# Two or one expert matrices in a ring slot instead of four slices, in a mixture-of-experts block on one core

## The chip, the core and the metric

One core of one Trainium2 chip runs the kernel as a single launch. The metric is device time in microseconds (us) of one execution; the median of three runs before the change is 612.62 us.

## What is computed

A residual stream `x` of 256 tokens by 1024 goes through a mixer, then through a mixture of 32 experts (top group, then two of its eight experts), then through a gated embedding and a final norm. All of it is float32. The part that the change touches is the mixture:

```python
for g in range(N_GROUPS):
    a = jnp.einsum('td,edf->tef', t, w_gate[g])
    b = jnp.einsum('td,edf->tef', t, w_up[g])
    hid = jax.nn.silu(a) * b * comb[:, g, :, None]
    y = y + jnp.einsum('tef,efd->td', hid, w_down[g])
```

Each expert has three matrices of 2 MB: gate and up are 1024 x 512, down is 512 x 1024. All 32 experts are read, 201 MB of the 225 MB that the kernel moves.

## The kernel before, in words

The 32 experts are worked on in eight **quads** of four (`QE`, `NQ`, lines 25 and 26). Up to 32 tokens of an expert stand in a block of 32 columns (`CAP`), so that the four experts of a quad fill 128 columns. A quad needs its gate weights (G), then its up weights (U), then its down weights (D), 8 MB each.

**Loads.** `load_w(q, i)` (line 430) fills one slot of 16 KB per partition, 2 MB in all, by one DMA: i = 0 to 3 are the gate slots, 4 to 7 the up slots, 8 to 11 the down slots. Before the change a slot holds all four experts of the quad, and of each expert two of the eight rows of a partition (`c:c + 2`, line 437), or one of four rows for down (line 439): in memory 4 KB in one run for each partition and expert. The loads go out on the queue of SyncE (SP), in program order. Slots come from the pool `ring` with six buffers (line 38); only the up slots of quad 0 lie elsewhere (pools `xr` and `x4`). A load waits on SP until the products that read its slot's earlier content are done. Two other users take slots of the ring: `wpp` (line 776), loaded after quad 2's down weights and read by the products of line 791, which follow quad 3's down products; and the gate matrix of the embedding (`load_gate`, line 657), which after quad 6 keeps two of the six slots to the end.

**Products.** `proj` (line 619) issues four products, one for each expert j, each into its own 32 columns of TensorE, so that the four run side by side. `gate_up` (line 624) calls it for c = 0 to 7, slot by slot: eight products (16 matmul records in the trace, since a float32 product leaves two) as soon as one slot has landed, and that slot is free after them. A matrix set is 32 products. `down` (line 647) does the same with four slots. After the gate products follow the up products, `hidden` and `hidden_t` (the activation and its transposes, `ph`), the down products, `combine` (the products `py`) and `spread` (the transposes `pc`). The gather of the next quad (`pgx`) lies between.

```python
for i in range(4):
    w = get_w(q, i0 + i).rearrange("p (e c f) -> p e c f", e=QE, c=2)
    for k in range(2):
        c = 2 * i + k
        proj(o, xg, c, w[:, :, k], c == 0, c == KC - 1)
    if filler:
        filler(i0 + i)
```

**Order around the change.** After quad 1's down loads, three gate loads of quad 2 are issued ahead (line 742, the third on the queue of GpSimd), and then comes a branch (line 747) that all engines pass, for rounds that these inputs don't need. In quad 7 the `filler` (line 716) puts the embedding's products `gate_x` between the expert products, and the down weights come by columns (`load_chunk`, line 823), which the change leaves alone.

Of the kernel before, what the change touches and what calls it, by code (L numbers as in the profile page):

```python
# [20 lines left out]
KC = D // P  # L21
FE = 512
NE = 32
CAP = 32
QE = 4
NQ = NE // QE
EPS = 1e-6
GELU_C = 0.044715
# [4 lines left out]
def hymba_conv_sgu_hmoe_block(ctx, tc, a):  # L33
    nc = tc.nc
# [19 lines left out]

# [1 line left out]
    sig0 = keep.tile([P, 1], F32, name="sig0")  # L56
# [29 lines left out]
    def keep_warm(n):  # L86
        pb = bank("warm")
        for _ in range(n):
# [6 lines left out]
                   allow_small_or_imprecise_dtypes=True)  # L95
    # lower[i, j] = 1 for j < i
    lower = keep.tile([P, 8, 8], F32, name="lower")
# [26 lines left out]

# [1 line left out]
    fy = tc.alloc_tile_pool(name="fy", bufs=1, side="left")  # L126
# [18 lines left out]
    load_in(1)  # L145
    # rows: g_sgu 0:4, w_conv 4:16, g_ple 16:24
    stage = fz.tile([24, P], F32, name="stage")
# [29 lines left out]

    # exact two-part splits of the weights, two pieces ahead of their products
    nsp = [0]
# [15 lines left out]

    # h^T, d = p * 8 + c, split in two exact parts
    hh = fz.tile([P, KC, NT * P], F32R, name="hh")
# [73 lines left out]
    vn = []  # L271
# [14 lines left out]

    # small parameters, spatial weights
    pst = bank("pst")
# [35 lines left out]

    # spatial mixing: mT[ch, t] = g_sgu[ch] * sum_s ws[t, s] vn[s, ch] + b[head, t]
    mT = fz.tile([P, 4, 256], F32, name="mT")
# [16 lines left out]
    def post_u():  # L343
        for i in range(2):
            gu = fz.tile([P, 512], F32, tag="g", name="gu", bufs=4)
            gelu(gu, pz_u[i])
            y = fz.tile([P, 512], F32, tag="g", name="yu", bufs=4)
            nc.vector.tensor_tensor(y, gu, mT[:, 2 * i:2 * i + 2].rearrange("p j n -> p (j n)"), op=OP.mult)
            put_y(4 + 2 * i, y)
        # router weights with the gain of the norm, bias on every partition  # L350
        gff3 = gffn.unsqueeze(2)
        pin(nc.vector.tensor_tensor(wr[:, :, 0:4], wgr, gff3.to_broadcast([P, KC, 4]), op=OP.mult))
        for g in range(4):
            pin(nc.vector.tensor_tensor(wr[:, :, 4 + 8 * g:12 + 8 * g], wrr[:, g],
                                        gff3.to_broadcast([P, KC, 8]), op=OP.mult))
        pbias = bank("pbias")
        nc.tensor.matmul(pbias[:, 0:36], ones_f, rb, start=True, stop=True)
        nc.vector.tensor_copy(biasB, pbias[:, 0:36])
# [16 lines left out]

# [1 line left out]
    po = [[bank("po", "L") for _ in range(2)] for _ in range(NT)]  # L377
# [48 lines left out]

# [1 line left out]
    wtiles = {}  # L428

    def load_w(q, i, queue=nc.sync):  # L430
        pool = ring if q or i < 4 or i > 7 else xr if i < 7 else x4
        w = slot(f"we{q}_{i}", pool)
        es = slice(q * QE, (q + 1) * QE)
        if i < 8:
            src = w_gate if i < 4 else w_up
            c = 2 * (i % 4)
            queue.dma_start(w.rearrange("p (e c f) -> p e c f", e=QE, c=2), src[:, es, c:c + 2, :])
        else:
            queue.dma_start(w.rearrange("p (e d) -> p e d", e=QE), w_down[:, es, i - 8, :])
        return w  # L440

    def get_w(q, i):
# [3 lines left out]

# [1 line left out]
    plog = bank("plog", "L")  # L448
# [17 lines left out]
    for t in range(NT):  # L466
        # normalized rows, d = p * 8 + c laid out as [c, p]
        nc.scalar.activation(h2[:, t].rearrange("t c p -> t p c"), xs[:, t].rearrange("t (p c) -> t p c", c=KC),
                             AF.Copy, scale=stat[:, 8 + t:9 + t])
    keep_warm(24)  # L470
    x4 = tc.alloc_tile_pool(name="x4", bufs=1, side="right")

# [1 line left out]
    gl = lg[:, :, 0:4]  # L474

    def ranks(v, n, name):
        """How many come before each of the n values: larger ones, or equal ones at a lower index."""
        shape = [P, NT, n, n]
        mine, other = v.unsqueeze(3).to_broadcast(shape), v.unsqueeze(2).to_broadcast(shape)
        gt = mp.tile(shape, F32, tag="gt", name="gt" + name)  # L480
        eq = mp.tile(shape, F32, tag="eq", name="eq" + name)
        nc.vector.tensor_tensor(gt, other, mine, op=OP.is_gt)
        nc.vector.tensor_tensor(eq, other, mine, op=OP.is_equal)
        nc.vector.tensor_tensor(eq, eq, lower[:, 0:n, 0:n].unsqueeze(1).to_broadcast(shape), op=OP.mult)
        nc.vector.tensor_tensor(gt, gt, eq, op=OP.add)
        rank = mp.tile([P, NT, n], F32, name="rank" + name)
        nc.vector.tensor_reduce(rank, gt, axis=AX.X, op=OP.add)
        return rank
# [61 lines left out]

    # combine weights
    gm = rout[:, :, 0:1]
# [33 lines left out]
    for t in range(NT):  # L586
        nc.vector.tensor_tensor(comb[:, t].rearrange("p (g e) -> p g e", g=4),
                                ohg[:, t].unsqueeze(2).to_broadcast([P, 4, 8]),
                                inner[:, t].unsqueeze(1).to_broadcast([P, 4, 8]), op=OP.mult)
    # rounds beyond the first that the fullest expert needs  # L590
    cmax = stat[:, 10:11]
# [5 lines left out]
    nc.vector.tensor_copy(nover, over[0:1, 7:8])  # L597
# [1 line left out]
    def hidden(pg, pu):  # L599
# [16 lines left out]
    def rows(j):  # L616
        return slice(j * CAP, (j + 1) * CAP)

    def proj(o, xg, c, w, first, last, placed=lambda i: i):
        for j in range(QE):  # L620
            placed(nc.tensor.matmul(o[rows(j)], xg[:, c, rows(j)], w[:, j], start=first, stop=last,  # L621
                                    tile_position=(0, j * CAP)))

    def gate_up(q, xg, filler=None):
        pg, pu = bank("pg"), bank("pu")
        for o, i0 in ((pg, 0), (pu, 4)):
            for i in range(4):
                w = get_w(q, i0 + i).rearrange("p (e c f) -> p e c f", e=QE, c=2)
                for k in range(2):
                    c = 2 * i + k  # L630
                    proj(o, xg, c, w[:, :, k], c == 0, c == KC - 1)
                if filler:
                    filler(i0 + i)
        return hidden(pg, pu)
# [12 lines left out]
    def down(q, hT, cm):  # L647
        pd = [bank("pd", "L") for _ in range(2)]
        for i in range(4):
            w = get_w(q, 8 + i).rearrange("p (e d) -> p e d", e=QE)  # L650
            for h in range(2):
                proj(pd[h], hT, i, w[:, :, h * 512:(h + 1) * 512], i == 0, i == 3)
        combine(pd, cm)

    # w_ple_gate, d = c * 128 + p, in two exact parts, and the gate's products with x as the first
    # seven quads leave it
    def load_gate():
        for i in range(2):
# [6 lines left out]
            for c in range(4):  # L665
                f = slice(c * D, (c + 1) * D)
                # with the gain of the norm before it
                g = cols[:, 16 + 4 * i + c:17 + 4 * i + c]
                nc.scalar.activation(hi[:, f], w[:, f], AF.Copy, scale=g)
                nc.vector.scalar_tensor_tensor(wlo[:, 4 * i + c], w[:, f], g, hi[:, f].bitcast(F32),  # L670
                                               op0=OP.mult, op1=OP.subtract)
# [34 lines left out]
    for q in range(NQ):  # L706
        if q:
            cm = spread(q, d)
        if q + 1 == NQ:
            # one token at most in each slot: its weight, and where it goes  # L710
            cmf = cm.rearrange("s t n -> s (t n)")
# [26 lines left out]
        if q == 1:  # L738
            # further rounds of CAP tokens per expert, as many as the fullest expert needs
            for i in range(3):  # L740
                # the loop uses no software queue, so nothing there waits for the last of these
                wtiles[q + 1, i] = load_w(q + 1, i, nc.gpsimd if i == 2 else nc.sync)
# [28 lines left out]
        if q == 2:  # L771
            # p @ w_ple_proj
            pq = tc.alloc_tile_pool(name="pq", bufs=1, side="right")
# [22 lines left out]

# [1 line left out]
    # The last quad's down weights arrive by columns.  # L798
    q = NQ - 1
# [83 lines left out]
    steps = {"D": down_chunk, "T": transposed, "Y": to_tokens, "S": gate_slots}  # L883
    # The columns' stages, so ordered that TensorE has products of one while another's are prepared.
    for step in "D0 T0 Y0 S0 D1 S1 T1 Y1 S2 D2 S3 T2 Y2 D3 S4 T3 Y3 D4 S5 T4 Y4 S6".split():
# [43 lines left out]
    added(*a11)  # L929
    # the gain goes on this half before its scale is known  # L930
    pin(nc.gpsimd.tensor_tensor(xs[:, 1, a10[2]], xs[:, 1, a10[2]], gF[:, a10[2]], op=OP.mult))
# [34 lines left out]
```

## Time and profile before

| What | Value |
|---|---|
| Median of three runs | 612.62 us (612.23 to 612.63) |
| Profiled execution, first to last instruction | 612.1 us |
| TensorE busy | 456.3 us (75%), 2955 matmul records |
| VectorE, ScalarE, GpSimd busy | 25%, 17%, 7% |
| Moved by DMA | 225.07 MB in 70600 packets, mean 368 GB/s |
| Mean granted TensorE clock | 0.871 of 2.4 GHz |

The span of the profiled execution stands 0.5 us under the median of the runs. The page cuts the span into 40 slices of 15.3 us; a digit is the busy share of a slice in tenths. In the rows of a timeline the first number is the start, the second the duration, and a bracket at the end tells how long the engine was idle before and what ended it.

### The profile page before, as it was taken

The numbers are of one execution on the slowest core, as the hardware profiler recorded it, in microseconds if no ns is written. First come the engines' busy times: TensorE is split into PE (matmuls) and PEld (weight loads), VectorE is DVE, ScalarE is ACT, GpSimd is POOL, SyncE is SP. The second block draws the span as 40 slices with busy tenths as digits, with TensorE's granted clock in tenths as the row PEclk, the third lists the DMA queues.
The fourth block names the chain that finished last, engine by engine and source line by source line (L and its number), as shares of the span: only waits on it lengthen the run. The fifth ranks groups of instructions, "written<-read, shape, count | busy, mean of one in ns | idle before, by whom it ended". The sixth has DMA issues, their size and how long they took to land.

```text
span 612.1 us, 6928 instructions
## 1 busy us (share of the span) xinstructions
PE 456.3 (75%) x2955; PEld 235.2 (38%) x2955; DVE 150.2 (25%) x275; ACT 101.9 (17%) x171; POOL 45.9 (7%) x42
## 2 busy tenths in 40 slices
PE   8999999989764775565657965756575676799891
PEld 8799988643310121121312331203110311356571
DVE  2647854422010201020012001200120012601236
ACT  4543545010000000000001200000000003300243
POOL 1543440000000000000000000000000000000003
PEclk9999999999875798788887998779877957899996
DMA  8997669699999799999999999999999999999921
GB/s 323 354 391 300 243 264 408 242 413 403 408 411 408 293 414 408 407 409 410 409 409 410 409 409 410 408 409 409 410 409 409 409 410 409 408 410 380 322 72 69
DMA packets 70600, 225.07 MB, mean 368 GB/s; under 512 B 3204, under 2 KB 15268, under 8 KB 70564
## 3 DMA queue, kind: packets, MB, share of 16 engines
q1 hardware_dynamic: 70036, 222.48, 93.3%
q0 software_dynamic: 528, 2.10, 0.9%
q8 instruction: 24, 0.39, 0.3%
q14 instruction: 12, 0.10, 0.0%
HBM read 223.52 MB, written 1.05 MB: 367 GB/s over the span
## 4 chain that ended last, share of the span: by engine, by line
DMA 43%; PE 19%; issue 1%; ACT 1%; DVE 1%; POOL 1%; POOLq 0%; SPq 0%; ACTq 0%
DMA we<-in_w_up_dram 17%; DMA we<-in_w_down_dram 16%; DMA we<-in_w_gate_dram 10%; PE pd L621 3%; PE pu L621 3%; PE pg L621 3%; PE pgg L688 1%; PE pgg L689 1%; PE py L644 1%; PE pj L791 1%; PE pgg L690 1%; PE pgg L880 1%; PE pyw L810 1%; PE pyw L811 1%; PE pyw L812 1%
## 5 line engine op out<-in xcount | busy, mean ns | idle before, releaser
L621 PE MATMUL pd<-we,hT 128*32 128x512 f32 x448 | 77.5, 833 | 45.4 <-DMA we<-in_w_down_dram 34.4
L621 PE MATMUL pu<-we,xg 128*32 128x512 f32 x512 | 70.9, 682 | 47.1 <-DMA we<-in_w_up_dram 47.1
L621 PE MATMUL pg<-we,xg 128*32 128x512 f32 x512 | 70.4, 690 | 27.4 <-DMA we<-in_w_gate_dram 27.4
L621 PEld LDWEIGHTS pd<-we,hT 128*32 128x32 f32 x448 | 14.5, 132 | 101.7 <-DMA we<-in_w_down_dram 59.1
L621 PEld LDWEIGHTS pu<-we,xg 128*32 128x32 f32 x512 | 15.2, 118 | 90.5 <-DMA we<-in_w_up_dram 47.2
L621 PEld LDWEIGHTS pg<-we,xg 128*32 128x32 f32 x512 | 15.8, 120 | 72.7 <-issue 36.9
L113 POOL TENSOR_TENSOR stat<-stat,mhalf 128x1 f32<-128x1 f32 (+1 forms) x9 | 6.0, 662 | 430.7 <-ACT yw L816 410.6
L249 PE MATMUL pz<-hh,wh 128*128 128x256 f32 x128 | 36.3, 283 | 0.7 <-ACT g L262 0.7
L251 PE MATMUL pz<-hl,wh 128*128 128x256 f32 x128 | 36.0, 281 | 0.0
L252 PE MATMUL pz<-hh,wl 128*128 128x256 f32 x128 | 35.9, 281 | 0.0
L530 PEld LDWEIGHTS pgx<-d,h 128*128 128x128 f32 x256 | 29.5, 192 | 11.1 <-issue 9.9
L530 PE MATMUL pgx<-d,h 128*128 128x128 f32 x256 | 31.7, 280 | 1.9 <-DVE d L519 1.9
L644 PE MATMUL py<-ys,cm 128*128 128x512 f32 x56 | 29.0, 662 | 2.8 <-DVE ys L639 2.8
L613 ACT ACTIVATE hT<-ph 128x512 f32<-128x512 f32 x8 | 4.8, 597 | 155.1 <-PE ph L611 155.1
L639 DVE COPY ys<-pd 128x512 f32<-128x512 f32 x7 | 4.8, 691 | 104.8 <-PE pd L621 104.8
L604 DVE TENSOR_TENSOR hp<-sg,pu 128x512 f32<-128x512 f32 x8 | 8.2, 1031 | 88.7 <-PE pu L621 88.7
L602 DVE TENSOR_TENSOR sg<-sg,pg 128x512 f32<-128x512 f32 x8 | 5.5, 688 | 97.6 <-ACT sg L601 97.6
L249 PEld LDWEIGHTS pz<-hh,wh 128*128 128x128 f32 x128 | 24.1, 188 | 1.1 <-ACT g L262 0.9
L252 PEld LDWEIGHTS pz<-hh,wl 128*128 128x128 f32 x128 | 24.1, 188 | 0.0
L251 PEld LDWEIGHTS pz<-hl,wh 128*128 128x128 f32 x128 | 24.1, 188 | 0.0
L638 ACT ACTIVATE ys<-pd 128x512 f32<-128x512 f32 x7 | 4.2, 597 | 110.4 <-PE pd L621 110.4
L601 ACT ACTIVATE sg<-pg 128x512 f32<-128x512 f32 x8 | 4.8, 598 | 101.0 <-PE pg L621 101.0
(233 smaller groups left out, 576.1 us busy)
## 6 DMA issues: line engine op xcount, KB each, us to landing
we<-in_w_up_dram SPq DMA_DIRECT2D x32, 2048.0 KB, 22.3
we<-in_w_gate_dram SPq DMA_DIRECT2D x31, 2048.0 KB, 18.5
we<-in_w_down_dram SPq DMA_DIRECT2D x28, 2048.0 KB, 24.0
wd<-in_w_down_dram SPq DMA_DIRECT2D x12, 512.0 KB, 9.3
wo<-in_w_out_dram SPq DMA_DIRECT2D x2, 2048.0 KB
wpg<-in_w_ple_gate_dram SPq DMA_DIRECT2D x4, 1024.0 KB
w_v<-in_w_in_dram SPq DMA_DIRECT2D x4, 512.0 KB, 7.3
w_c<-in_w_in_dram SPq DMA_DIRECT2D x2, 1024.0 KB
```

The costliest lines, as they stand in the source:

```text
L249: nc.tensor.matmul(o, wh[:, s], hh[:, c], start=(c == 0 and j % 2 == 0), stop=False, skip_group_check=True)
L251: nc.tensor.matmul(o, wh[:, s], hl[:, c], start=False, stop=False, skip_group_check=True)
L252: nc.tensor.matmul(o, wl[:, s], hh[:, c], start=False, stop=last, skip_group_check=True)
L530: nc.tensor.matmul(pg[:, c * P:(c + 1) * P], h2[:, t, 4 * i + c], d[:, t].rearrange("p e s -> p (e s)"), start=(t == 0), stop=(t == NT - 1))
L604: nc.vector.tensor_tensor(hp.rearrange("s c p -> s p c"), sg.rearrange("s (p c) -> s p c", c=4), pu.rearrange("s (p c) -> s p c", c=4), op ...
L621: placed(nc.tensor.matmul(o[rows(j)], xg[:, c, rows(j)], w[:, j], start=first, stop=last, tile_position=(0, j * CAP)))
L644: nc.tensor.matmul(py, cm[:, t], ys[:, f], start=True, stop=True)
L688: nc.tensor.matmul(pgg[t][h], hi[:, s], wh[:, f], start=first, stop=False)
L689: nc.tensor.matmul(pgg[t][h], hi[:, s], wl[:, f], start=False, stop=False)
L690: nc.tensor.matmul(pgg[t][h], lo[:, s], wh[:, f], start=False, stop=last)
L791: nc.tensor.matmul(pj, pT[:, c, t * P:(t + 1) * P], wv[:, c, f], start=(c == 0), stop=(c == 1))
L810: pin(nc.tensor.matmul(pyw[h], yh_, wh[:, f], start=(k == 0), stop=False))
```

## The change

A table `PER` gives each quad the number of experts in a slot: two for quads 0, 6 and 7, one for quads 1 to 5. With two, a slot holds four rows c of each expert (two for down), 8 KB in one run; with one, a slot holds the whole matrix of one expert, 16 KB in one run. Number and size of the loads, their order and the number of products stay. A new generator `granules` hands out the rows c in order, each with its four experts' weights: with two experts to a slot it takes two slots at a time, with one it takes all four. `proj` takes a list of four weights. The filler is called at the same places as before. Comments were dropped too.

```diff
+PER = [2] + [1] * (NQ - 3) + [2] * 2
...
     def load_w(q, i, queue=nc.sync):
         pool = ring if q or i < 4 or i > 7 else xr if i < 7 else x4
         w = slot(f"we{q}_{i}", pool)
-        es = slice(q * QE, (q + 1) * QE)
+
+        EP = PER[q]
+        CP = KC // EP
+        g, n = divmod(i % 4, QE // EP)
+        es = slice(q * QE + n * EP, q * QE + (n + 1) * EP)
         if i < 8:
             src = w_gate if i < 4 else w_up
-            c = 2 * (i % 4)
-            queue.dma_start(w.rearrange("p (e c f) -> p e c f", e=QE, c=2), src[:, es, c:c + 2, :])
+            c = CP * g
+            queue.dma_start(w.rearrange("p (e c f) -> p e c f", e=EP, c=CP), src[:, es, c:c + CP, :])
         else:
-            queue.dma_start(w.rearrange("p (e d) -> p e d", e=QE), w_down[:, es, i - 8, :])
+            c = CP // 2 * g
+            queue.dma_start(w.rearrange("p (e c d) -> p e c d", e=EP, c=CP // 2), w_down[:, es, c:c + CP // 2, :])
         return w
+
+    def granules(q, i0, c_slot):
+
+        EP = PER[q]
+        for g in range(EP):
+            ws = [get_w(q, i0 + g * (QE // EP) + n).rearrange("p (e c f) -> p e c f", e=EP, c=c_slot)
+                  for n in range(QE // EP)]
+            for k in range(c_slot):
+                yield g * c_slot + k, [ws[j // EP][:, j % EP, k] for j in range(QE)]
...
-            placed(nc.tensor.matmul(o[rows(j)], xg[:, c, rows(j)], w[:, j], start=first, stop=last,
+            wj = w[j] if isinstance(w, list) else w[:, j]
+            placed(nc.tensor.matmul(o[rows(j)], xg[:, c, rows(j)], wj, start=first, stop=last,
                                     tile_position=(0, j * CAP)))
...
         for o, i0 in ((pg, 0), (pu, 4)):
-            for i in range(4):
-                w = get_w(q, i0 + i).rearrange("p (e c f) -> p e c f", e=QE, c=2)
-                for k in range(2):
-                    c = 2 * i + k
-                    proj(o, xg, c, w[:, :, k], c == 0, c == KC - 1)
-                if filler:
-                    filler(i0 + i)
+            for c, w in granules(q, i0, KC // PER[q]):
+                proj(o, xg, c, w, c == 0, c == KC - 1)
+                if filler and c % 2:
+                    filler(i0 + c // 2)
...
-        for i in range(4):
-            w = get_w(q, 8 + i).rearrange("p (e d) -> p e d", e=QE)
+        for i, w in granules(q, 8, 4 // PER[q]):
             for h in range(2):
-                proj(pd[h], hT, i, w[:, :, h * 512:(h + 1) * 512], i == 0, i == 3)
+                proj(pd[h], hT, i, [r[:, h * 512:(h + 1) * 512] for r in w], i == 0, i == 3)
```

## Rows read from the trace of the kernel before

**Rows 1.** The page, busy tenths in 40 slices of the span.

```profile
PEclk9999999999875798788887998779877957899996
DMA  8997669699999799999999999999999999999921
GB/s 323 354 391 300 243 264 408 242 413 403 408 411 408 293 414 408 407 409 410 409 409 410 409 409 410 408 409 409 410 409 409 409 410 409 408 410 380 322 72 69
```

**Rows 2.** The page, the chain that ended last, by engine.

```profile
DMA 43%; PE 19%; issue 1%; ACT 1%; DVE 1%; POOL 1%; POOLq 0%; SPq 0%; ACTq 0%
```

**Rows 3.** Products of TensorE, timeline, quad 3's gate and up, and quad 2's up.

```profile
274.08 3.38 PE L621 MATMUL pg<-we,xg 128*32 128x512 f32 x16 [3.08 <-DMA we<-in_w_gate_dram]
279.21 1.92 PE L621 MATMUL pg<-we,xg 128*32 128x512 f32 x16 [1.75 <-DMA we<-in_w_gate_dram]
284.33 3.38 PE L621 MATMUL pg<-we,xg 128*32 128x512 f32 x16 [3.20 <-DMA we<-in_w_gate_dram]
...
224.22 1.92 PE L621 MATMUL pu<-we,xg 128*32 128x512 f32 x16 [3.20 <-DMA we<-in_w_up_dram]
```

**Rows 4.** DMA packets: whole span, 32 to 42, 350 to 450, 562 to 570 us.

```profile
DMA packets 70600, 225.07 MB, mean 368 GB/s; under 512 B 3204, under 2 KB 15268, under 8 KB 70564
...
DMA packets 1976, 3.87 MB, mean 387 GB/s; under 512 B 709, under 2 KB 717, under 8 KB 1975
...
DMA packets 10286, 40.92 MB, mean 409 GB/s; under 512 B 306, under 2 KB 306, under 8 KB 10282
...
DMA packets 2803, 2.78 MB, mean 348 GB/s; under 512 B 86, under 2 KB 2803, under 8 KB 2803
```

**Rows 5.** Timeline, SP's loads: quad 3 down; `wpp`; the first after quad 0's products.

```profile
287.79 19.10 SPq L439 DMA_DIRECT2D we<-in_w_down_dram  x4
...
246.39 1.29 SPq L777 DMA_DIRECT2D wpp<-in_w_ple_proj_dram  x1
...
118.49 2.08 SPq L439 DMA_DIRECT2D we<-in_w_down_dram  x2
```

**Rows 6.** Issue to landing: `we` in 350 to 450; issues of 60 to 70, 118 to 119.

```profile
DMA to landing us min/median/max: 23.8/24.0/24.1
...
we<-in_w_gate_dram SPq DMA_DIRECT2D x1, 2048.0 KB, 8.6
...
we<-in_w_down_dram SPq DMA_DIRECT2D x1, 2048.0 KB, 8.8
```

**Rows 7.** Timeline of TensorE, products in a row: quad 0's gate, quad 2's gate.

```profile
116.51 7.07 PE L621 MATMUL pg<-we,xg 128*32 128x512 f32 x64
...
210.27 0.66 PE L543 MATMUL pc<-ident,d 128*128 128x128 f32 x2 [4.11 <-PEq L747]
210.86 7.71 PE L621 MATMUL pg<-we,xg 128*32 128x512 f32 x48
```

**Rows 8.** Stretches of 1 us: engines' busy time, then PEclk, DMA share, GB/s.

```profile
529.00:530.00 1.00, 1.00 (x9) 0.14 (x2) 1.00 (x1) 0.00 (x0) 0.00 (x0) 0.66 1.03 414
530.00:531.00 1.00, 0.96 (x9) 0.73 (x9) 0.66 (x4) 0.38 (x1) 0.00 (x0) 1.00 1.01 401
```

**Rows 9.** Timeline of TensorE after quad 3's down products, 325 to 341 us.

```profile
333.59 7.13 PE L791 MATMUL pj<-wpp,pT 128*128 128x512 f32 x16 [0.69 <-ACT pT L785]
```

**Rows 10.** Timeline, end of quad 1: last down products, the next load on SP.

```profile
199.23 3.27 PE L621 MATMUL pd<-we,hT 128*32 128x512 f32 x16 [5.81 <-SPq L747]
...
210.39 0.40 SPq L437 DMA_DIRECT2D we<-in_w_gate_dram  x1
```

**Rows 11.** The chain that ended last, in order of time, quad 7.

```profile
509.48 16.81 DMA we<-in_w_gate_dram
526.42 3.51 PE pg L621 x16
...
534.03 1.85 PE pg L621 x16
...
548.51 1.85 PE pu L621 x16
```

## The prediction, on record before the run

> **What bounds the kernel now.** I read the page first. Its slices show DMA as the resource that is never off from about 122 to 550 us: the busy digit is 9 and the rate 403 to 414 GB/s in every slice but one [rows 1]. The chain agrees: 43% of the span is DMA, 19% TensorE [rows 2]. The timeline then shows how that looks inside a quad: eight products every 5.12 us (274.08, 279.21, 284.33), each group after a wait for its weights [rows 3]. 5.12 us is what one load of 2048 KB takes at 409 GB/s [rows 4]. SP issues a load as soon as a slot is free: quad 3's first down load starts at 287.79 [rows 5], 0.1 us after the eight gate products at 284.33 end (3.38 us) [rows 3]. So one slot is being read, up to five are in flight, and a load lands 24.0 us after its issue [rows 6], more than four loads' time. This lead keeps DMA busy through branch-free quads. The end is different: from 526.42 on TensorE works almost without a wait, and the quad 7 gate load that lands there sets when this stretch begins [rows 11].
>
> **What the change does to a load.** Bytes, loads, order and products are the same. Packets get longer. Three stretches have loads with runs of 1, 2 and 4 KB: 348, 387 and 409 GB/s [rows 4]. On each of 16 engines a packet then takes 47.1, 84.7 and 160 ns, so 37.6 ns for each KB and 9.5 ns beside it. By this line 8 KB take 310 ns and 16 KB 611 ns: a load takes 4.96 us in quads 6 and 7 and 4.88 us in quads 1 to 5, in place of 5.12. Ends: 5.12 (no gain beyond 4 KB) and 4.80 (nothing beside the 37.6 ns). I take the line, because three rows lie on it. Were all else hidden, this would be 60 loads by 0.24 and some 20 by 0.16, about 17 us.
>
> **What it does to the slots.** With one expert to a slot no product but the first three can run before the fourth slot has landed, since every row c needs all four experts in order. And no slot is free before the last four of the 32 products. So four of six slots stand full while the burst runs, and only two loads are in flight. The count from the landing of the fourth load:
>
> The burst. 32 products at full clock took 7.1 us in quad 0 [rows 7]. But now TensorE waits over 10 us before each burst. After a wait of 4.11 us (ahead of two transposes), 24 products of quad 2 took 7.71 us, so 32 take 9.5 (7.71 and a quarter of 7.07) [rows 7]. After 3.79 us of wait, at 526.42 [rows 11], the clock stood at half until 529.7 (0.66 in the mean over 529 to 530, then 1.00) [rows 8]; 3.3 us at half rate cost 1.6 us, which gives 8.7. Ends: 7.1 and 13.5 (four groups at the 3.38 us of a cold one [rows 3]). I take 8.7 rather than 9.5, since a wait of 3.20 us was once followed by a group at full speed, 1.92 us at 224.22 [rows 3]. The Trainium skill ("TensorE: Matmul & The Clock Gate", HAM oscillation) says that a DMA wait between groups of products sends the clock back to half and that every group then starts cold. By that rule it is 8.7 to 9.5 in each burst; by the row at 224.22 alone it would be 7.1 and the sum below 22.7 us less.
>
> The restart. A load that met an empty queue landed 8.6 and 8.8 us after its issue [rows 6], 3.5 us beyond its 5.12; with the shorter transfer 8.4.
>
> Six slots free for experts: loads one and two are in flight. The first expert's slot is free 0.7 us before the burst ends, so load three goes out at 8.0, lands at 16.4, and load four at 21.3. Before, four loads took 20.5. Each handover from one matrix set to the next costs **0.8 us** instead of gaining 1.0. There are ten: G to U and U to D of quads 1, 2, 4 and 5, and D to G of 4 to 5 and 5 to 6: 8.0.
>
> Five slots: `wpp` is loaded behind quad 2's down weights (issue at 246.39 [rows 5]) and is read until 340.7 by products that follow quad 3's down products [rows 9]. Through quad 3 one slot is gone. Then one load is in flight at the burst, and two, three and four follow it: 8.0, 16.4, 21.3, 26.1. Each costs **5.7 us**; G3 to U3, U3 to D3 and D3 to G4: 17.1. In D2 to G3 the 1.25 MB of `wpp` and the embedding input (3.2 us) lie in the queue too: 26.1 against 23.7 before, 2.4.
>
> **The other parts.** Quad 0 with two to a slot: the ring's first slot is free after 16 products, not eight, 119.6 instead of 118.49 [rows 5], with DMA idle; quad 1's first two loads win half of it back: 0.6. Quad 1's end: 32 products instead of eight lie between the last down load and the branch, 5.4 us more (8.7 against 3.27), and the third early load, on GpSimd's queue, now waits for that burst. But the eight products at 199.23 came after a wait of 5.81 us for the branch and not for data [rows 10], and the longer burst uses up that time. Ends 0 and 5.4; I take 0.5, because the row shows the cover. If the cover is gone, the load at 210.39 [rows 10] and all behind it are that much later. Quad 6: eight loads by 0.16 in the two handovers left, minus 1.3. Quad 7: its first products now need two landed slots, not one, so the stretch at 526.42 begins one load later, plus 5.0. Two slots of the ring are gone there too: the first pair is free at 535.9 (534.03 and 1.85 [rows 11]) plus 5.0, its successors land 8.4 and 5.0 later, at 554.3, and the up products want them at 548.51 plus 5.0: 0.8 late. Together 5.8. SP's own issue times (19.10 us for four loads [rows 5]) shrink with the packets and stay behind DMA; `proj`'s list adds no instruction: nothing.
>
> **Sum.** 8.0 + 17.1 + 2.4 + 0.6 + 0.5 - 1.3 + 5.8 = 33.1 us. The profiled span is 612.1, which makes 645.2; the median stands 0.5 above the span: **646 us**.
>
> **Rivals.**
> *Slot of `wpp` not in the way* (its products moved ahead, into quad 3's waits). For: TensorE will have 10 us waits there, and the gather `pgx` is already placed between up groups. Against: before, `pj` came only after quad 3's down products, though waits of 3 us lay ahead of it [rows 3, 9]. The three handovers fall from 5.7 to 0.8: 14.7 less, 631 us.
> *The longer runs bring nothing*, the change doing half of what it says. Load time 5.12: handovers cost 1.2 and 6.4, D2 to G3 3.1, no gain in quad 6: about 9 more, 655 us. Against it stand the three rates on one line.
> *The clock doesn't come back within a burst.* Burst 13.5: 4.8 more in each of 14 handovers, 713 us. Against: rows 8 show it back after 3.3 us of work.
> *Faster: the two loads in flight outlast the burst.* This happens in the handovers of quads 1 to 6. It decides where the burst takes under 7.9 us (then the fourth load lands within 20.5) and the ring has six slots throughout. At 7.1 each of 13 handovers gains 0.8, and 10.4 less 0.8 (D2 to G3) and 5.6 (the rest) leave a gain of 4.0: 608.6 us. For it speaks the row at 224.22, against it the waits, three times as long as that one, and `wpp`.
>
> **How the numbers follow.** The forecast has 0.54, `wpp` free 0.14, no gain from length 0.13, cold bursts 0.06, faster 0.11, and 0.02 is left for something else. The range runs from the warm burst with `wpp` held (10 us over the span, 622) to the burst of 9.5 with no gain from length (666). It holds `wpp` free and the unchanged rate and leaves out the cold and the faster case, some 0.18. A measurement of this kernel can tell 0.2% from no change. All cases but one are slower: faster 0.11, same 0.03, slower 0.86.
>
> **What would show it.** Packets: 47,104 of 4 KB become 8,192 of 8 KB and 7,680 of 16 KB, so the page should have 39,368. The rate should be near 429 GB/s while two loads are in flight, with a dip once in each 21 us in quads 1 to 5 and a long one, some 6 us, in quad 3. Products should come in groups of 64 records of 8 to 9.5 us. Loads three and four of a set should land 8 to 14 us after issue, not 24. Quad 7's first gate products should wait for a second load. I am wrong if the DMA slices of quads 2, 4 and 5 stay at 9 with over 420 GB/s, if TensorE reads an expert's slot as it lands, or if bursts run at full clock from the start.

## The result, and the profile after

The changed kernel takes 642.78 us (median of four runs, 640.97 to 646.13) against 612.62 us (612.23 to 612.87): a ratio of 1.0503, 95% interval 1.047 to 1.0537. It is slower by 5%, and its runs lie 5 us apart where those of before lie within 0.6 us. The profiled execution has a span of 639.7 us and took 641.43 us.

First the page of the kernel after, the same slices as [rows 1], then its packets and the chain by engine, as [rows 2]:

```profile
PEclk9999999997899789869589898879778986899897
DMA  8997589599999999896787999998999999989911
GB/s 316 346 394 317 200 356 423 221 405 425 364 378 374 423 381 378 349 426 243 326 340 293 428 369 388 421 414 328 389 422 400 421 422 412 421 342 385 329 38 66
DMA packets 39368, 225.07 MB, mean 352 GB/s; under 512 B 3204, under 2 KB 15268, under 8 KB 23460
...
DMA 33%; PE 28%; DVE 2%; issue 1%; ACT 1%; POOL 1%; SPq 0%; POOLq 0%; ACTq 0%; DVEq 0%
```

Before, quads 2 to 6 had one rate, 407 to 414 GB/s. Now single slices reach 421 to 428, above all of before, and beside them stand slices of 243 to 390. DMA got faster while it works and has gaps that it didn't have. In the chain TensorE's share has grown from 19 to 28% and DMA's has fallen from 43 to 33%: some of the time in which weights were moving all along is now spent on products with hardly a load moving beside them.

The timeline of TensorE, kernel after (start, duration, count of records, the wait before):

```profile
218.02 8.32 PE L637 MATMUL pg<-we,xg 128*32 128x512 f32 x57 [2.01 <-DMA we<-in_w_gate_dram]
...
286.58 8.49 PE L637 MATMUL pg<-we,xg 128*32 128x512 f32 x57 [2.98 <-DMA we<-in_w_gate_dram]
...
313.21 9.25 PE L637 MATMUL pu<-we,xg 128*32 128x512 f32 x58 [2.97 <-DMA we<-in_w_up_dram]
...
339.80 7.05 PE L637 MATMUL pd<-we,hT 128*32 128x512 f32 x52 [1.39 <-DMA we<-in_w_down_dram]
...
351.61 7.13 PE L803 MATMUL pj<-wpp,pT 128*128 128x512 f32 x16 [0.69 <-ACT pT L797]
...
493.10 5.90 PE L637 MATMUL pg<-we,xg 128*32 128x512 f32 x26 [4.42 <-DMA we<-in_w_gate_dram]
...
533.50 6.61 PE L637 MATMUL pd<-we,hT 128*32 128x512 f32 x24 [2.09 <-DMA we<-in_w_down_dram]
```

In quads 1 to 5 nearly all 64 records of a set now stand in one burst that begins with the landing of the fourth load; the groups of 16 every 5.12 us [rows 3] are gone. (493.10 and 533.50 are sets of quad 6, with two experts to a slot.) Around the burst of 286.58 the stretches of 3 us (busy times, then granted clock, DMA share, GB/s) and SP's issues read:

```profile
287.00:290.00 3.00, 3.00 (x17) 0.59 (x13) 0.00 (x0) 0.00 (x0) 0.00 (x0) 0.50 0.79 339
290.00:293.00 3.00, 3.00 (x32) 0.92 (x28) 0.00 (x0) 0.00 (x0) 0.00 (x0) 0.94 0.03 11
293.00:296.00 3.00, 3.00 (x25) 1.04 (x18) 0.00 (x0) 0.46 (x1) 0.00 (x0) 1.00 0.31 66
296.00:299.00 3.00, 3.00 (x30) 3.00 (x28) 0.69 (x1) 0.13 (x1) 0.00 (x0) 1.00 0.82 317
```

```profile
294.69 1.28 SPq L442 DMA_DIRECT2D we<-in_w_up_dram  x3
296.06 1.36 SPq L445 DMA_DIRECT2D we<-in_w_down_dram  x1
```

DMA stands at 11 and 66 GB/s for 6 us while TensorE works at full load. SP issues the next loads at 294.69, as the burst ends (286.58 + 8.49 = 295.07) and its first slot comes free. The first 3 us of the burst run at 0.50, the lower level of the clock. The three up loads issued there landed 8.7, 13.2 and 17.6 us later, not 24 [rows 6].

To see where the time went I compare the landing of the same last load of a set. Here are three groups of the kernel before that begin with one, to be held against 218.02, 493.10 and 533.50 above:

```profile
219.09 1.92 PE L621 MATMUL pg<-we,xg 128*32 128x512 f32 x16 [0.53 <-DMA we<-in_w_gate_dram]
...
468.78 3.32 PE L621 MATMUL pg<-we,xg 128*32 128x512 f32 x16 [2.52 <-DMA we<-in_w_gate_dram]
...
510.97 1.92 PE L621 MATMUL pd<-we,hT 128*32 128x512 f32 x16 [1.56 <-DMA we<-in_w_down_dram]
```

| Stretch, up to the last load of | Before | After | Lost | Predicted |
|---|---|---|---|---|
| start to quad 2 gate | 219.1 | 218.0 | -1.1 | 2.7 |
| to quad 6 gate (12 handovers) | 249.7 | 275.1 | 25.4 | 25.9 |
| to quad 6 down | 42.2 | 40.4 | -1.8 | -1.3 |
| to the end of the span | 101.1 | 106.2 | 5.1 | 5.8 |
| span | 612.1 | 639.7 | 27.6 | 33.1 |

The predicted column is the sum's own terms: 0.6, 0.5 and two handovers in the first line; eight handovers of 0.8, 17.1 and 2.4 in the second.

### The profile page after: what moved, and what is told of

Same layout as the page of the kernel before. It is cut to its first block, busy times and chain, and to the rows that moved or that the text cites. A ratio compares the mean times of both kernels' runs of the same rounds, so it can differ in the third digit from the quotient of the medians.

```text
span 639.7 us, 6928 instructions
## 1 busy us (share of the span) xinstructions
PE 489.0 (76%) x2955; PEld 245.8 (38%) x2955; DVE 149.7 (23%) x275; ACT 101.7 (16%) x171; POOL 45.7 (7%) x42
## 2 busy tenths in 40 slices
DMA packets 39368, 225.07 MB, mean 352 GB/s; under 512 B 3204, under 2 KB 15268, under 8 KB 23460
## 3 DMA queue, kind: packets, MB, share of 16 engines
HBM read 223.52 MB, written 1.05 MB: 351 GB/s over the span
## 4 chain that ended last, share of the span: by engine, by line
DMA 33%; PE 28%; DVE 2%; issue 1%; ACT 1%; POOL 1%; SPq 0%; POOLq 0%; ACTq 0%; DVEq 0%
DMA we<-in_w_down_dram 13%; DMA we<-in_w_gate_dram 11%; DMA we<-in_w_up_dram 9%; PE pg L637 7%; PE pu L637 7%; PE pd L637 7%; DVE wlo L682 1%; PE pgg L702 1%; PE pgg L700 1%; PE pgg L701 1%; PE pgg L892 1%; PE pyw L822 1%; PE pgx L545 1%; PE pyw L823 1%; PE pyw L824 1%
## 5 line engine op out<-in xcount | busy, mean ns | idle before, releaser
L637 PE MATMUL pu<-we,xg 128*32 128x512 f32 x512 | 87.8, 681 | 41.8 <-DMA we<-in_w_up_dram 41.8
L637 PE MATMUL pd<-we,hT 128*32 128x512 f32 x448 | 87.0, 654 | 39.6 <-DMA we<-in_w_down_dram 28.2
L637 PE MATMUL pg<-we,xg 128*32 128x512 f32 x512 | 87.1, 712 | 33.1 <-DMA we<-in_w_gate_dram 33.1
L637 PEld LDWEIGHTS pd<-we,hT 128*32 128x32 f32 x448 | 19.8, 115 | 101.8 <-issue 43.4
L637 PEld LDWEIGHTS pu<-we,xg 128*32 128x32 f32 x512 | 19.9, 123 | 95.3 <-DMA we<-in_w_up_dram 51.2
L637 PEld LDWEIGHTS pg<-we,xg 128*32 128x32 f32 x512 | 19.4, 126 | 91.0 <-issue 45.1
L545 PEld LDWEIGHTS pgx<-d,h 128*128 128x128 f32 x256 | 29.5, 192 | 11.2 <-issue 8.5
L657 PE MATMUL py<-ys,cm 128*128 128x512 f32 x56 | 26.2, 608 | 1.4 <-DVE ys L652 1.4
## 6 DMA issues: line engine op xcount, KB each, us to landing
we<-in_w_gate_dram SPq DMA_DIRECT2D x31, 2048.0 KB, 10.8
```

The lines of the kernel that those rows point to most:

```text
L545: nc.tensor.matmul(pg[:, c * P:(c + 1) * P], h2[:, t, 4 * i + c], d[:, t].rearrange("p e s -> p (e s)"), start=(t == 0), stop=(t == NT - 1))
L637: placed(nc.tensor.matmul(o[rows(j)], xg[:, c, rows(j)], wj, start=first, stop=last, tile_position=(0, j * CAP)))
L657: nc.tensor.matmul(py, cm[:, t], ys[:, f], start=True, stop=True)
```

## The experiments

The theory: a set's slots are held to the end of its burst, so too few loads are in flight, and DMA stands idle from the landing of the last of them until the next set's loads have started up. The rivals: length and order alone cost the time, or the clock does. Times of the kernel before beside these runs are 612.9 to 613.1 us.

**1. Hold the slots without longer runs.** The kernel before, its loads of 4 KB unchanged; in quads 1 to 5 the products of a set go round all four slots, so that none is free before the last round.

```diff
+    def hold(o, xg, cw, first, last):
+        for r in range(4):
+            for i, (c, w) in enumerate(cw):
+                j = (i + r + 1) % 4
+                nc.tensor.matmul(o[rows(j)], xg[:, c, rows(j)], w[:, j], start=first and r == 0,
+                                 stop=last and r == 3, tile_position=(0, j * CAP))
```

> The kernel before, loads and packets unchanged (4 KB runs), but in quads 1 to 5 the 32 products of a set go through all four slots in turn, so that none can start before the fourth slot has landed (but three) and every slot is read until the last four products. Theory (held slots): handovers as in the changed kernel with loads of 5.12 us: 21.7 us in place of 20.5 with six slots (ten times), 25 to 27 us in quad 3 (three times), 3 for wpp's place: 641 to 650 us, DMA gaps in every handover. Rival (the long packets are slow or badly fed): no packet is longer, 612 to 616 us.

659.99 us (651.99 to 661.71), ratio 1.0727 (1.0654 to 1.0799). The rival, that the longer packets are what costs and holding costs nothing, is out: holding alone loses 47 us, more than the whole change. The size was missed. The bursts of quad 2 show by how much:

```profile
222.55 9.10 PE L628 MATMUL pg<-we,xg 128*32 128x512 f32 x58 [5.78 <-DMA we<-in_w_gate_dram]
...
245.95 9.69 PE L628 MATMUL pu<-we,xg 128*32 128x512 f32 x58 [3.40 <-DMA we<-in_w_up_dram]
...
269.49 9.87 PE L628 MATMUL pd<-we,hT 128*32 128x512 f32 x52 [2.08 <-DMA we<-in_w_down_dram]
```

They take 9.1 to 9.9 us, against 8.32, 8.63 and 7.05 us in the same sets of the changed kernel, and the fourth loads are 23.4 and 23.5 us apart. So the loss is the slots', and longer runs are not needed for it.

**2. Give `wpp` a buffer of its own.** The changed kernel, with one line other:

```diff
-            wv = slot("wpp")[:, 0:2048].rearrange("p (c n) -> p c n", c=2)
+            wv = pq.tile([P, 2, D], F32, name="wpp")
```

> The changed kernel, with wpp in a buffer of its own instead of a ring slot. Theory: quad 3's handovers fall from 26.6, 26.6 and 24.8 us to about 21.5, some 14 us, and a little at D2 to G3: 625 to 631 us. Rivals (packets, or TensorE's clock alone): loads, packets and products are the same, 640 to 645 us.

630.81 us (626.82 to 632.66), ratio 1.0283 (1.0237 to 1.0329): 12.0 us less than the changed kernel, where the prediction's rival had 14.7 for three handovers. Quad 3:

```profile
286.17 8.22 PE L637 MATMUL pg<-we,xg 128*32 128x512 f32 x57 [2.98 <-DMA we<-in_w_gate_dram]
...
307.42 9.97 PE L637 MATMUL pu<-we,xg 128*32 128x512 f32 x58 [3.46 <-DMA we<-in_w_up_dram]
...
329.89 8.75 PE L637 MATMUL pd<-we,hT 128*32 128x512 f32 x52 [2.98 <-DMA we<-in_w_down_dram]
```

The fourth loads are 21.3 and 22.5 us apart, not 26.6 and 26.6: one slot is worth about one load time in each handover. The second is over 21.3 by about what its burst of 9.97 us is over 8.7.

**3. Two more slots.** The changed kernel; in quads 2 to 5 the fourth load of each set goes to a pool of two further slots.

```diff
+        if i % 4 == 3 and 2 <= q <= 5:
+            pool = x5[0]
...
+            x5.append(tc.alloc_tile_pool(name="x5", bufs=2, side="right"))
```

> The changed kernel, with two more slots in quads 2 to 5 (the fourth load of each set goes to a second pool of two), packets and bursts unchanged. Theory: a whole next set is in flight while a burst runs, so sets of quads 2 to 5 land every 19.5 us at 429 GB/s without gaps; 11 handovers that took 254 us with wpp take about 218: 604 to 610 us. Rival (packets): no change, 640 to 645. Rival (TensorE's cold bursts bound it): no change either, 640 to 645.

613.31 us (611.19 to 616.54, ten runs), ratio 1.0003 (0.9988 to 1.0017). 29.5 of the 30.2 us come back with nothing changed but the number of slots. Yet it stayed 3 us short of what I expected. With free slots the scheduler had put products of quad 2's up set before the gate burst:

```profile
221.92 1.04 PE L640 MATMUL pu<-we,xg 128*32 128x512 f32 x2 [1.15 <-DMA we<-in_w_up_dram]
...
227.06 6.60 PE L640 MATMUL pg<-we,xg 128*32 128x512 f32 x57 [0.32 <-issue]
```

An up load had gone out at 208.85, ahead of the last gate load, and that one only at 216.33; this burst began at 227.06, 9 us later than in the changed kernel. And `wpp` still took a slot in quad 3, where fourth loads are 21.7 and 22.4 us apart. From quad 4's up set to quad 5's down set, with all eight slots, they are 19.6 us apart, four loads' time, as the theory wants, though the bursts there take 8.4 to 9.2 us.

**4. Two experts in the middle, four at both ends.** The changed kernel, one table:

```diff
-PER = [2] + [1] * (NQ - 3) + [2] * 2
+PER = [4] + [2] * (NQ - 2) + [4]
```

> PER is 2 in quads 1 to 6 and 4 (slots as before the change) in quads 0 and 7. Theory: 16 products hold two slots for 3.5 to 5.3 us while four are in flight, so DMA never runs dry; 72 loads by 0.16 us less: 599 to 604 us, landings 4.96 us apart. Rival (longer packets are slow): between 612 and 640. Rival (no gain from length): 612.

603.03 us (601.96 to 605.0), ratio 0.9842 (0.9814 to 0.987): 1.6% faster than before. The page:

```profile
GB/s 319 343 388 341 217 262 408 269 418 407 422 420 420 293 426 419 417 422 421 420 423 421 421 419 422 420 422 421 421 423 419 424 419 407 404 410 374 323 42 70
```

The stretch of quads 2 to 6 is without a gap again, at 417 to 426 GB/s. Two slots become free in the middle of a set, and four loads in flight outlast what is left of it. The gain is the rate's: 60 loads in quads 2 to 6 by 0.16 us (5.12 less 4.96) make 9.6 us, and 10.0 were measured. I had counted 72 loads, quad 1's too (11.5 us); there DMA has gaps as before (293 GB/s in one slice).

**5. Forty-four dummy products ahead of each set**, to keep the clock up:

```diff
+        if EP == 1:
+            keep_warm(44)
```

> The changed kernel with 44 products of 128x128 that nobody reads ahead of every set of quads 1 to 5 (some 9.5 us of TensorE's wait), so that the burst starts at full clock. Slots, loads and packets unchanged. Theory (the burst's length sets when load three goes out): bursts of about 7.0 us in place of 8.3 to 9.3, each six-slot handover 1.3 to 2 us shorter, 12 to 20 us in all: 623 to 631 us. Rival (the clock is beside the point): 640 to 645. Rival (TensorE has no time for them): over 645.

657.85 us (656.33 to 658.71), ratio 1.0726 (1.0705 to 1.0748). The mean granted clock rose from 0.887 to 0.962, and the second rival held, that TensorE has no time for them:

```profile
217.08 11.39 PE L90 MATMUL warm<-ident 128*128 128x128 f32 x86
...
228.41 7.07 PE L639 MATMUL pg<-we,xg 128*32 128x512 f32 x64
```

The burst takes 7.07 us, but without a wait before it: the dummies ended after the weights had landed. As a test of the clock this run decides nothing; it shows that TensorE has no 11 us to give here.

**6. Two experts in every quad:**

```diff
-PER = [2] + [1] * (NQ - 3) + [2] * 2
+PER = [2] * NQ
```

> PER is 2 in all eight quads; against the kernel with 4 in quads 0 and 7 (603.0 us) only quads 0 and 7 differ. Theory: quad 7's products begin one load later, 5.0 to 6.0 us, quad 0 0.6: 608 to 610 us. Rival (the filler covers the wait for the second slot): 602 to 605.

607.11 us (605.73 to 608.69), ratio 0.9896 (0.9876 to 0.9916): 4.1 us over run 4, which differs in quads 0 and 7 only. The change's choice for the two ends costs about 4 us, in place of 6.4 (0.6 and 5.8) by the prediction.

**7. What the runs point to:** four experts to a slot in quads 0 and 7, two in 1 and 6, one in 2 to 5 with the two slots of run 3 and `wpp` of run 2.

```diff
+PER = [4, 2, 1, 1, 1, 1, 2, 4]
```

> PER is 4, 2, 1, 1, 1, 1, 2, 4; two more slots in quads 2 to 5 and wpp outside the ring. Theory: no handover of quads 2 to 5 runs dry, 48 loads of 4.88 us and 24 of 4.96 instead of 72 of 4.96: 3.8 us under the 603.0 of two experts to a slot, 597 to 601, DMA slices of quads 2 to 5 at 425 GB/s or more. Rival (two in flight beyond the set are still not enough): 605 to 615.

599.34 us (598.68 to 599.92), ratio 0.9773 (0.9757 to 0.979): faster than both kernels. The page has 412 to 432 GB/s from quad 2's up weights to the end of quad 5:

```profile
GB/s 316 344 388 353 210 262 408 251 406 411 420 421 427 319 412 429 418 430 426 429 426 428 425 432 423 431 426 428 426 419 420 422 419 410 408 410 373 321 51 70
```

Here the length of a burst no longer matters. The fourth loads of these three sets are 19.6 us apart, after bursts of 8.24 and 9.11 us, as after one of 7.05 us at 376.90:

```profile
396.47 8.24 PE L640 MATMUL pg<-we,xg 128*32 128x512 f32 x57 [3.85 <-DMA we<-in_w_gate_dram]
...
416.06 9.11 PE L640 MATMUL pu<-we,xg 128*32 128x512 f32 x58 [3.87 <-DMA we<-in_w_up_dram]
...
435.64 7.05 PE L640 MATMUL pd<-we,hT 128*32 128x512 f32 x52 [3.01 <-DMA we<-in_w_down_dram]
```

**8. Ten dummy products that fill the last wait.** They read the third expert's slot, so they cannot start before it has landed.

```diff
+            if warm and first and j == 2:
+                pb = bank("warm")
+                for _ in range(10):
+                    nc.tensor.matmul(pb[:, 0:P], ident, wj[:, 0:P], start=True, stop=True)
```

> Ten dummy products of 128 columns stand behind the third expert's first product in each gate and up set of quads 1 to 5. They read that expert's slot, so they run in the 4.9 us between the third and the fourth landing, when TensorE otherwise waits. Theory (the clock's fall in the wait sets part of the burst, and the burst sets when the third load goes out): the ten gate and up bursts, 8.3 to 9.3 us in the changed kernel, take 7.1 to 7.5; the set after each comes 1.2 to 1.9 us sooner; 12 to 19 us less in all, 624 to 631 us. Rival 1 (the restart of the loads alone decides, the clock isn't on the path): bursts shorter but 640 to 645 us. Rival 2 (the dummies stand in the way of other products, as the 44 did): over 645 us. If bursts stay above 8.3 us, the clock isn't what makes them long.

644.73 us (639.35 to 646.52), ratio 1.0498 (1.0458 to 1.0539). Quad 2:

```profile
218.06 3.34 PE L642 MATMUL warm<-we,ident 128*128 128x128 f32 x20
221.33 6.62 PE L637 MATMUL pg<-we,xg 128*32 128x512 f32 x57
...
237.46 3.86 PE L642 MATMUL warm<-we,ident 128*128 128x128 f32 x20
241.16 2.62 PE L545 MATMUL pgx<-d,h 128*128 128x128 f32 x22
243.71 7.05 PE L637 MATMUL pu<-we,xg 128*32 128x512 f32 x58
```

The time is the first rival's (640 to 645), but by the second one's mechanism: the bursts are as short as the theory wants, and no wait stands before them. Dummies, and the gather that the scheduler put behind them, end after the landing and cost what the bursts save (8.3 to 6.6 us, 8.6 to 7.05 us).

**9. Six dummies, in gate sets alone.** As run 8 with `range(6)`, and only where `pg` is computed.

> Six dummy products, and in the gate sets of quads 1 to 5 alone, so that none stands in front of the gather in an up set. After a cold first product of the third expert (1.9 us) six take about 2.4 us, which ends before the fourth landing. Theory (the clock is on the path through the third load's issue): the gate bursts that took 8.3 to 8.7 us in the changed kernel take 6.6 to 7.1, their ends and the issue of the next set's third load come 1.3 to 2.0 us sooner after the landing, in five handovers: 6 to 10 us less, 633 to 637 us; quad 3's gate set to up set about 24.5 us between the fourth landings in place of 26.6. Rival (the saving is given back, by the loads' restart or by what follows the burst): 641 to 645 us though the gate bursts are short.

642.97 us (640.15 to 646.17), ratio 1.05 (1.0471 to 1.053): the rival's number, though in quad 3 all went as the theory has it:

```profile
286.38 2.17 PE L642 MATMUL warm<-we,ident 128*128 128x128 f32 x12
289.43 6.62 PE L637 MATMUL pg<-we,xg 128*32 128x512 f32 x57 [0.88 <-DMA we<-in_w_gate_dram]
...
314.30 9.03 PE L637 MATMUL pu<-we,xg 128*32 128x512 f32 x58 [3.33 <-DMA we<-in_w_up_dram]
...
340.65 7.05 PE L637 MATMUL pd<-we,hT 128*32 128x512 f32 x52 [1.50 <-DMA we<-in_w_down_dram]
```

This burst is 1.9 us shorter than in the changed kernel, and the next fourth load follows after 24.9 us in place of 26.6. So within a handover the clock is on the path. But over quads 1 to 5 the five gate bursts sum to 35.2 us in place of 43.3, and the ten up and down bursts to 89.3 in place of 80.3: 124.5 against 123.6 in all. What the gate sets gained, the sets after them lost; quad 2's down burst took 8.75 us in place of 7.05. The handovers follow: from quad 2's gate to quad 6's gate, the four from gate to up set came 1.6 to 2.1 us sooner and the four from down to gate set 0.4 to 1.6 us later. Why the later bursts grew is open: I have one profile of each, and no run that changes the up sets alone.

## Why the prediction was right

It said 646 us, slower, and 642.78 was measured.

**The load.** Right. 39,368 packets, as reckoned. Of the loads after, those of 16 KB land 4.88 us apart (303.42, 308.28, 313.17), those of 8 KB in quad 7 some 4.97 us apart (553.62, 558.6, 563.55). Both are the line's values; neither end of the bound (5.12, 4.80) was met. One of the line's three points was misread, though: in the stretch of 387 GB/s [rows 4] 709 of 1976 packets are under 512 B, and the 1259 of 2 KB and more hold 3 KB in the mean, not 2. The other two rows give the same line without it. And the rival without a gain from length adds up to some 8 us, not 9: 654 us.

**The slots.** Right, and the heart of it: runs 1, 2 and 3 take it from three sides. The twelve handovers from quad 2's gate to quad 6's gate took 275.1 us; eight of 21.3 and four of 26.1 make 274.8. That it fits this closely is luck: the eight took 1.9 us more than forecast (172.3) and the four 1.7 us less (102.7). One by one they scatter: 20.9 to 22.5 with six slots (21.3 forecast), 24.7, 26.6, 26.6 and 24.8 where `wpp` holds one (26.1). `wpp` did hold its slot to 358.7, the end of the products at 351.61.

**The burst.** 8.7 us was one value for unlike ones (8.2 in the mean of fifteen): 8.3 to 9.3 in gate and up sets, 7.05 in four of five down sets, where bursts ran at full clock from the start, one of the prediction's own signs of being wrong. Quad 2's down set:

```profile
256.99 3.21 PE L637 MATMUL pd<-we,hT 128*32 128x512 f32 x4 [4.54 <-DMA we<-in_w_down_dram]
261.87 7.05 PE L637 MATMUL pd<-we,hT 128*32 128x512 f32 x52 [1.68 <-DMA we<-in_w_down_dram]
```

The prediction had TensorE wait over 10 us before each burst. But the first products of the first three experts run as their loads land, and no wait before a burst was longer than 3.9 us. Before these four, the records of the third expert took 3.2 to 3.5 us, with a shorter wait (1.4 to 1.7 us, before the other eleven 1.9 to 3.9) between them and the burst. The wait alone does not decide it: in run 7 the burst at 435.64 took 7.05 us after 3.01. The Trainium skill ("TensorE: Matmul & The Clock Gate", HAM oscillation) describes a kernel in which a long wait for DMA before each group sends the clock back to half, so that every group starts cold. The gate and up bursts agree (0.50 granted over 287 to 290), the down bursts at 7.05 us do not start cold (1.00 granted over 339.8 to 342).

By the sum's way a burst of 7.05 us shortens its handover by some 1.6 us. With five slots it did (24.7 and 24.8 against 26.6). With six, the handover after quad 4's down burst took 21.4 us all the same, where that way gives 19.7; this stays unexplained.

**Quad 0 to the branch.** The step that was off. 2.7 us were forecast, and the last gate load of quad 2 landed 1.1 us sooner. Of these 3.8 us, 1.9 are a start of the first expert products at 114.6 instead of 116.51 [rows 7]. Run 2, the same kernel up to there, starts them at 116.12, so most of that is scatter between executions, not the change. The rest is the branch, and there the prediction misread the row at 199.23 [rows 10]: its 5.81 us were a wait for data. Kernel before, the early gate load on GpSimd's queue, and what the two queues (q0 GpSimd's, q1 SP's) moved in 188 to 198 us (packets, MB, share of the time of 16 DMA engines):

```profile
183.69 0.96 POOL L437 DMA_DIRECT2D we<-in_w_gate_dram  x1 [79.55 <-PE pd L621]
...
q0 software_dynamic: 501, 2.05, 51.3%
q1 hardware_dynamic: 507, 2.01, 50.7%
```

That load took half of what DMA moved while quad 1's last down load and two gate loads stood on SP's queue. In the kernel after it went out only with the end of quad 1's down burst:

```profile
203.86 0.76 POOL L442 DMA_DIRECT2D we<-in_w_gate_dram  x1 [100.49 <-PE pd L637]
...
207.16 0.35 SPq L442 DMA_DIRECT2D we<-in_w_gate_dram  x1
```

So quad 1's last down products start at 197.01 instead of 199.23, and the last packet of SP's queue had moved at 206.33 instead of 209.17. The second row is the load at 210.39 of [rows 10], the first that SP issues behind the branch: 3.2 us sooner. In all eleven profiles it follows 0.8 to 1.2 us after the last packet on SP's queue. By this timing SP passes the branch when its own loads are through, not when TensorE's burst is; the term took the branch as passed no earlier (its ends were 0 and 5.4), on the row of TensorE. Of the 3.2 us, 2.2 went again: with GpSimd's load moving beside it this load landed 10.8 us after its issue, not 8.7.

**Quad 7.** Right in size (5.1, forecast 5.8); its cause is not shown. The products do want the second slot, which landed at 553.62, after a first at 548.7. But the chain that ended last runs over VectorE:

```profile
548.42 4.87 DVE wlo L682 x4
553.28 0.33 DVE wsl L725
...
554.20 0.50 PE pgg L702
...
556.54 3.56 PE pg L637 x28
```

The split of the embedding's gate matrix ends at 553.28, within 0.4 us of that landing, and the embedding's products go first. Before, eight expert products stood in that time, from 526.42 to 529.93 [rows 11]; now only the first slot's two could. No run takes the two apart: in run 6 the split ends at 520.48 and the second slot lands at 520.71. The 0.8 for a late pair of up loads did not occur.

**The faster rival.** It hung on bursts under 7.9 us and six free slots throughout. Four down bursts met the first, too few to carry it; run 7 reaches its end, loads in flight that outlast the burst, by two slots more: 599 us. The forecast came out 3 us high by two errors that partly cancel. The span was 5.5 us under the sum's 645.2, most of it the 3.8 us of the first stretch; and the median stands 3.1 us above the profiled span, where 0.5 was taken over from the kernel before.

## What to carry to other kernels

Before a load is made longer, count when its slot comes free, and from that how many loads are in flight in the longest stretch that holds them. They must outlast that stretch and the start-up of the next load (here 8.7 us of burst, and 3.6 us, what 8.5 from issue to landing are over the 4.88 of a load's time); one slot fewer cost about one load time, 5 us, in each handover. The longer run itself was a true gain, and two experts to a slot (8 KB) took most of it without a byte more of memory.

## What the runs showed that I had not expected

- The same 32 products take 7.05 us in one burst and 8.3 to 9.3 in another, and what goes before a burst goes with it. But in run 9 making five bursts faster left the sum of all fifteen about as it was (124.5 and 123.6 us), and with slots enough (runs 3 and 7) a burst's length costs nothing.
- Holding slots with 4 KB runs (run 1) gave longer bursts, 9.0 us in the mean of fifteen against 8.2 in the changed kernel; its down sets took 7.05 to 10.0. Why is open.
- The changed kernel varies more from run to run: 5 us, and 10 us in run 1, where 0.6 us lay between the runs of before beside the changed kernel and 1.2 us between those of run 7.
- A row of a timeline that sums up several issues can hold waits. SP in run 4, with 8 KB:

```profile
304.66 19.69 SPq L442 DMA_DIRECT2D we<-in_w_gate_dram  x4
```

The four issues start at 304.66, 312.30, 313.12 and 323.98 and take 0.37 us each; the rest is SP waiting for slots. With 4 KB, the four of [rows 5] took 3.6 to 4.9 us each, 17.5 of their 19.10. So SP's own time did shrink with the packets, as the prediction has it. It bounds nothing here, since DMA was busy all along.
